# When the last step of the attention state's second half is put down: both head pairs together, or one pair at a time

## The chip, the cores and the metric

The kernel runs on one core of a Trainium2 chip. The core has engines with a queue of instructions each: TensorE (PE, matrix products into PSUM banks), VectorE (DVE), ScalarE (ACT), GpSimd (POOL) and SyncE (SP), whose queue issues nearly all of this kernel's transfers. They wait for each other through semaphores. The metric is the device time of one execution in microseconds (us).

## The reference

One block of a streaming encoder, for 1024 tokens of width 1024 and 16 meta tokens ahead of them: a mixer of a multi-scale pooling branch and a chunked, gated linear attention (GLA, 4 heads, chunks of 64), merged by sigmoid gates, and then an MLP with a squared ReLU. The part that bears on the change:

```python
def gla_chunk_step(S, inp):
    qc, kc, vc, ac = inp
    ...
    o = jnp.einsum('bhts,bhsv->bhtv', scores, vc) + jnp.einsum('bhtk,bhkv->bhtv', qc * jnp.exp(b), S)
    ...
    return S_new, o

    o = gla_chunked(q, k, v, log_a)
    o = rmsnorm(o, gla_norm.reshape(GLA_HEADS, GLA_DV)) * jax.nn.silu(r).reshape(B, L, GLA_HEADS, GLA_DV)
    y_b = jnp.einsum('blc,cd->bld', o.reshape(B, L, GLA_VAL), w_gla_out)
    m = jax.nn.sigmoid(ga) * y_a + jax.nn.sigmoid(gb) * y_b
    return jnp.einsum('bld,de->ble', m, w_out)
```

All of it is float32.

## The kernel before

A float32 operand is split into a rounded part and a remainder, and every product is made of three matmuls (`mm3`, L280 to L282: rounded by rounded, and the two mixed ones). Weights go through a ring of two slots (`Ring`, W1): a load from DRAM into one of two raw buffers (L118, on SP), the rounding on ACT (L84, writes `w1h`), the remainder on DVE (L85, writes `w1l`).

The program has two parts, `one` (norm, projections, the pooling branch) and `rest` (GLA across the chunks, merge, output projection, MLP). The change is in `gla()`, the first long step of `rest`. There the 1024 tokens are two halves of 512, and the 4 heads two pairs. `across(p, half)` is a generator for one pair in one half. It yields four times, so it has five steps: turning the keys (L1124), the state's updates (L1130, L1136), the scores by the values (L1144), the queries by the states with the norm (L1154 to L1164), and the last one, which the change is about (L1167 to L1175): eight transposes on PE (L1168) into two PSUM banks (`m2` for pair 0, `sc` for pair 1), the product with the gate `sr` on DVE (L1169), the rounding into `yg` on ACT (L1171) and its remainder on DVE (L1172). Each of these DVE and ACT operations is 128x1024.

Between the steps PE does filler work, which `drive` hands out in units of three matmuls of 128x512, at a cost of 0.64 each: `pour(us)` takes units until their costs reach `us`, and a surplus is carried over. The filler is first the products of the pooling branch, `ya_block`, and then `yb_block(j, 0)`, y_b of half 0. Block j (of four) has the weights of 256 columns of w_gla_out and makes the output tiles d = 2j and 2j + 1, twelve matmuls each, into one of three `mm` PSUM banks in turn. I call these tiles d0 to d7. DVE leaves a tile's bank with L1095 (gate times product), adds the pooling branch (L1096), ACT rounds the sum (L1099), and DVE makes the remainder (L1100). The gates and the pooling branch come in small buffers (`o`, `t1`, `c`, loads L1037).

At the end of `gla()` the rest of the filler is done. `merge_open` then reuses the memory, and `yb_block(j, 1)` follows, half 1's tiles in the order of blocks 2, 3, 0, 1. Blocks 2 and 3 still lie in the two ring slots; block 0's and 1's weights are loaded again. Between them the weights w_out come in four loads (L1237, into `acc`) with a rounding (L1238) and a remainder (L1239), since the output projection (`out_tile`) begins after half 1's d0 and d1.

PE runs in the order in which the program is written. The other engines' orders are set by a scheduler that works from PE's order.

Of the kernel before, what the change touches and what calls it, by code (L numbers as in the profile page):

```python
# [122 lines left out]
def kernel(  # L123
# [30 lines left out]
    def bank(tag):  # L154
        if tag == "sc":
            sc_n[0] += 1
            return two("sc")[:, sc_n[0] % 2]
        return psp[tag].tile([P, 512], F32, name=f"b_{tag}", tag=tag)

    def two(tag):  # L160

        if tag in ("sc", "gs"):
            if tag not in wide:
                wide[tag] = psp[tag].tile([P, 2, 512], F32, name=f"b_{tag}", tag=tag)
            return wide[tag]
        return psp[tag].tile([P, 2, 512], F32, name=f"b_{tag}", tag=tag)
# [45 lines left out]
    def f32(ap):  # L212
        return ap.bitcast(F32)
# [11 lines left out]
    def inv_sqrt(ss, n, inv, bias=None):  # L225

        rows, cols = ss.shape[0], n
        k = inv_sqrt.k = (inv_sqrt.k + 1) % 2
        v, y = stat[2 * k][:rows, 0:cols], stat[2 * k + 1][:rows, 0:cols]
        t = stat[2 * k][:rows, 8 : 8 + cols]  # L230
        act.activation(y, ss, ACT.Ln, scale=inv, bias=eps_t[:rows] if bias is None else bias)
        dve.tensor_scalar(v, ss, inv, EPS if bias is None else bias, ALU.mult, ALU.add)
        act.activation(y, y, ACT.Exp, scale=-0.5)
        if cols == 1:
            dve.scalar_tensor_tensor(t, v, y, y, ALU.mult, ALU.mult)
        else:
            dve.tensor_tensor(t, v, y, ALU.mult)
            dve.tensor_tensor(t, t, y, ALU.mult)
        dve.tensor_scalar(t, t, -0.5, 1.5, ALU.mult, ALU.add)
        dve.tensor_tensor(ss, y, t, ALU.mult)  # L240
        return ss
# [74 lines left out]
    def drive(steps, late=0.0):  # L316

        due = late
        for n, (ring, aps, fn) in enumerate(steps):
            if fn is not start:  # L320
                for r in rings:
                    if late and r.loaded >= r.used + len(aps):
                        r.ask()
                    else:
                        r.top_up()
            wbs = [ring.views.pop(ring.used + i) for i in range(len(aps))] if ring else []
            held = len(aps)
            if ring:
                ring.used += held
            for cost in fn(*wbs) or ():  # L330
                if cost == "keep":
                    held = 0
                    continue
                if cost == "free":
                    if ring:
                        ring.done, held = ring.done + held, 0
                    else:
                        W1.done += 1
                    due = late if n < 3 else 1.0
                    for r in rings:  # L340
                        r.ask()
                        if not late:
                            r.split()
                    continue
                if late and cost != "wait":
                    due -= cost
                    if due <= 0:
                        for r in rings:
                            r.split(pin=True)
                yield cost  # L350
            if ring:
                ring.done += held
# [155 lines left out]
    def quad(a):  # L508
        return a.rearrange("p (k c) -> p k c", k=4)
# [384 lines left out]
    def part(i):  # L894
        return slice(i * CH, (i + 1) * CH)
# [15 lines left out]
    def dec_of(p, half):  # L911
        return decs[:, (2 * half + p) * NC : (2 * half + p + 1) * NC]
# [99 lines left out]
    def fetch(p, half):  # L1012
        if half < 2:
            nc.sync.dma_start(S["gi"][p], gi_dram[p, half])
# [96 lines left out]
    def across(p, half):  # L1111


        gi, kt, W = S["gi"][p], S["kt"][p], S["W"][p]
        scc = gi[:, 0].rearrange("p (e j t) -> p e j t", e=2, j=4)
        kl, qe = gi[:, 1], gi[:, 2]
        v = S["v"][:, p, 4 * half : 4 * half + 4].rearrange("p j (e c) -> p j e c", e=2)
        dec = dec_of(p, half)
        first = S["S"][:, half, p]
        wide2 = lambda: two("sc" if p else "m2")  # L1120
        sr = S["sr"][p].rearrange("p e t -> p (e t)")
        b = quad(bank("ms") if p == 0 else wide2()[:, 0])
        for j in range(4):
            pe.transpose(b[:, j], kl[:, j * P : (j + 1) * P], ident)  # L1124
        act.activation(kt, b, ACT.Copy)
        yield 1.4
        kv = wide2().rearrange("p u (j c) -> p u j c", j=4)
        for j in range(4):
            for u, e in ((0, 0), (1, 1), (1, 0), (0, 1)):
                pe.matmul(  # L1130
                    kv[part(e), u, j], kt[part(u), j, part(e)], v[part(u), j, e], start=True, stop=True,
                    tile_position=(u * CH, e * CH),
                )
        states = [first] + [W[:, c] for c in range(NC - 1)] + ([S["S"][:, 1, p]] if half == 0 else [])
        for c, dst in enumerate(states[1:]):
            dve.scalar_tensor_tensor(dst, states[c], dec[:, c : c + 1], kv[:, c % 2, c // 2], ALU.mult, ALU.add)  # L1136
        nc.sync.dma_start(S["sr"][p], r_dram[2 * p : 2 * p + 2, half].rearrange("h p t -> p h t"))
        yield 5.0

        o = wide2().rearrange("p e (j c) -> p e j c", j=4)  # L1140
        for j in range(4):
            for e in range(2):
                for u in range(2):
                    pe.matmul(  # L1144
                        o[part(u), e, j], scc[part(u), e, j], v[part(u), j, e], start=j == 0, stop=False,
                        tile_position=(u * CH, u * CH), skip_group_check=True,
                    )

        dve.tensor_copy(rms[p][:, :2], o[:, :, 3, P - 1])
        yield 0.8  # L1150
        for j in (3, 0, 1, 2):
            for e, u in ((0, 0), (1, 1), (1, 0), (0, 1)):
                c = 2 * j + u
                pe.matmul(  # L1154
                    o[part(u), e, j], qe[part(e), part(c)], states[c][part(e)], start=False, stop=True,
                    tile_position=(e * CH, u * CH), skip_group_check=True,
                )
        fetch(p, half + 1)
        on, o = S["on"][p], o.rearrange("p e j c -> p (e j) c")
        act.activation(on, o, ACT.Square)  # L1160
        ss = rms[p]
        dve.tensor_reduce(ss, on, AX.X, ALU.add)
        rs = inv_sqrt(ss, 8, 1.0 / P)
        dve.tensor_tensor(on, o, rs[:, :, None].broadcast_to([P, 8, P]), ALU.mult)  # L1164
        yield 8.0
        b = wide2().rearrange("p e (j c) -> p (e j) c", j=4)
        for j in range(8):  # L1167
            pe.transpose(b[:, j], on[:, j], ident)  # L1168
        dve.tensor_tensor(sr, b.rearrange("p a c -> p (a c)"), sr, ALU.mult)  # L1169
        yh, yl = (S["yg"][half][:, n, 2 * p : 2 * p + 2].rearrange("p e t -> p (e t)") for n in range(2))  # L1170
        act.activation(yh, sr, ACT.Copy)  # L1171
        dve.tensor_tensor(yl, sr, f32(yh), ALU.subtract)  # L1172
        done.add((p, half))
        if {(0, half), (1, half)} <= done:
            done.add(("o", half))  # L1175

    def gla():
        W1.far = len(W1.queue)
        filler = drive(fill, 5.0)

        owed = [0.0]

        def pour(us):
            owed[0] += us
            while owed[0] > 0:
                cost = next(filler, None)
                if cost is None or cost == "wait":
                    owed[0] = 0.0
                    return
                owed[0] -= cost  # L1190

        pour(OPENING)
        for half in range(2):
            live = [across(p, half) for p in range(2)]
            while live:
                waits = [(g, next(g, None)) for g in live]
                live = [g for g, w in waits if w is not None]
                pour(max([w for _, w in waits if w is not None], default=2.0) * PACE)
        for _ in filler:
            pass  # L1200

    step(rest, gla)


# [426 lines left out]
```

## Time and profile before

| | |
|---|---|
| Time, median of 3 runs | 1226.18 us (1223.92 to 1226.18) |
| The profiled execution's own time | 1222.42 us |
| Its span, first to last instruction | 1220.6 us |
| PE busy | 1204.6 us (99%) |
| DVE busy | 838.9 us (69%) |
| ACT busy | 572.3 us (47%) |
| Granted TensorE clock, mean | 0.999 |

A time in a row of the timeline is a start, counted from the span's start, and the number behind it is the duration. Matmuls overlap: a row of 0.39 us does not keep the next one from starting 0.23 us later, so the pace is read from the starts. An arrow in brackets names what ended an idle time; where an instruction waits for several, it is the one that came last by the profile. SPq rows are issues of transfers; the transfer itself lands some microseconds later.

### The profile page before, as it was taken

To read this page: it belongs to the slowest core of one execution; us is meant where nothing else is said; L and a number is where in the kernel's file an instruction comes from. 1 tells how busy PE (TensorE), PEld (TensorE's weight loads), DVE (VectorE), ACT (ScalarE), POOL (GpSimd) and SP (SyncE) were. 2 spreads that over 40 slices of the span, in tenths; PEclk is the share of its full clock that TensorE was granted. 3 is DMA by queue.
4 is the path that set the end of the run, shared out by engine and by line. 5 is a ranking of instruction groups with operands and counts; after the bars stand their busy time and mean duration, and the time that the engine had idled before them with its cause. 6 is when DMAs were issued, how large, how long until landed. Compare 5 with 4: busy or idle time off the path is not lost.

```text
span 1220.6 us, 18363 instructions
## 1 busy us (share of the span) xinstructions
PE 1204.6 (99%) x6807; PEld 996.5 (82%) x6807; DVE 838.9 (69%) x1381; ACT 572.3 (47%) x1009; POOL 75.7 (6%) x96
## 2 busy tenths in 40 slices
PE   9999999999999999999999999999999999999997
PEld 7988977777778887888778888888888888888886
DVE  7536557565777569735887677676775887887686
ACT  8536444444456224314655455454554444444544
POOL 0000053322230000000000000000000000000000
PEclk9999999999999999999999999999999999999999
DMA  8213334435338967821244454444569973333532
GB/s 261 73 35 114 104 95 137 141 104 166 96 121 291 326 222 248 296 67 69 104 139 156 143 162 152 148 155 145 173 228 322 334 246 104 96 95 96 171 96 87
DMA packets 153355, 192.76 MB, mean 158 GB/s; under 512 B 12177, under 2 KB 88225, under 8 KB 153266
## 3 DMA queue, kind: packets, MB, share of 16 engines
q1 hardware_dynamic: 153266, 191.59, 48.9%
q8 instruction: 53, 0.87, 0.3%
q14 instruction: 36, 0.29, 0.1%
HBM read 128.62 MB, written 62.93 MB: 157 GB/s over the span
## 4 chain that ended last, share of the span: by engine, by line
PE 89%; DVE 4%; DMA 3%; ACT 1%; issue 1%; POOL 0%; SPq 0%; DVEq 0%; ACTq 0%; POOLq 0%
PE b_mm L280 7%; PE b_mm L282 7%; PE b_mm L281 7%; PE b_y L280 6%; PE b_y L282 6%; PE b_y L281 6%; PE b_oa L281 5%; PE b_oa L282 5%; PE b_oa L280 5%; PE b_z L280 4%; PE b_z L282 4%; PE b_z L281 4%; PE b_sc L280 4%; PE b_ob L281 4%; PE b_ob L282 4%; PE b_ob L280 4%
## 5 line engine op out<-in xcount | busy, mean ns | idle before, releaser
L685 ACT ACTIVATE w1h<-raw 128x512 fp32r<-128x512 f32 x106 | 65.9, 623 | 57.9 <-PE b_y L281 25.3
L686 DVE TENSOR_TENSOR w1l<-raw,w1h 128x512 fp32r<-128x512 f32 x106 | 72.5, 685 | 20.5 <-ACT w1h L685 20.5
L280 PE MATMUL b_sc<-th,w1h 128*128 128x512 f32 x216 | 85.7, 397 | 0.7 <-ACT u2p L1414 0.7
L280 PE MATMUL b_z<-th,w1h 128*128 128x512 f32 x216 | 85.3, 395 | 0.6 <-DVE c L804 0.4
L281 PE MATMUL b_sc<-tl,w1h 128*128 128x512 f32 x216 | 84.9, 393 | 0.0
L281 PE MATMUL b_z<-tl,w1h 128*128 128x512 f32 x216 | 84.3, 391 | 0.4 <-DVE tl L1300 0.4
L282 PE MATMUL b_sc<-th,w1l 128*128 128x512 f32 x216 | 84.5, 391 | 0.0
L685 ACT ACTIVATE w1h<-fs 128x512 fp32r<-128x512 f32 x81 | 51.1, 631 | 71.1 <-PE b_y L281 33.2
L282 PE MATMUL b_z<-th,w1l 128*128 128x512 f32 x216 | 84.2, 390 | 0.0
L686 DVE TENSOR_TENSOR w1l<-fs,w1h 128x512 fp32r<-128x512 f32 x81 | 56.9, 702 | 25.9 <-ACT w1h L685 25.8
L280 PE MATMUL b_mm<-th,w1h 128*128 128x512 f32 (+1 forms) x208 | 72.2, 347 | 0.0
L281 PE MATMUL b_mm<-tl,w1h 128*128 128x512 f32 (+1 forms) x208 | 71.1, 342 | 0.0
L282 PE MATMUL b_mm<-th,w1l 128*128 128x512 f32 (+1 forms) x208 | 71.1, 342 | 0.0
L685 ACT ACTIVATE w1h<-bt 128x512 fp32r<-128x512 f32 x46 | 29.1, 632 | 70.9 <-issue 43.9
L1490 DVE TENSOR_TENSOR bt<-w,w 128x512 f32<-128x512 f32 x80 | 54.7, 684 | 0.7 <-DMA w<-in_w_ff_dram 0.6
L280 PE MATMUL b_mm<-wo,th 128*128 128x512 f32 x128 | 50.4, 394 | 0.0
L282 PE MATMUL b_mm<-wo,tl 128*128 128x512 f32 x128 | 50.0, 390 | 0.0
L281 PE MATMUL b_mm<-wo,th 128*128 128x512 f32 x128 | 49.9, 390 | 0.0
L280 PE MATMUL b_y<-wo,w1h 128*128 128x512 f32 x128 | 49.9, 389 | 0.0
L282 PE MATMUL b_y<-wo,w1l 128*128 128x512 f32 x128 | 49.8, 389 | 0.0
L281 PE MATMUL b_y<-wo,w1h 128*128 128x512 f32 x128 | 49.8, 389 | 0.0
L686 DVE TENSOR_TENSOR w1l<-bt,w1h 128x512 fp32r<-128x512 f32 x46 | 31.8, 691 | 25.6 <-ACT w1h L685 25.6
(405 smaller groups left out, 3331.8 us busy)
## 6 DMA issues: line engine op xcount, KB each, us to landing
hf_dram<-h SPq DMA_DIRECT2D x112, 256.0 KB, 2.1
raw<-hf_dram SPq DMA_DIRECT2D x112, 256.0 KB, 2.6
w<-in_w_ff_dram SPq DMA_DIRECT2D x64, 256.0 KB, 4.7
raw<-in_w_in_dram SPq DMA_DIRECT2D x22, 512.0 KB, 4.7
raw<-in_w_ff_dram SPq DMA_DIRECT2D x16, 512.0 KB, 4.2
rawx<-in_w_ff_dram SPq DMA_DIRECT2D x16, 512.0 KB, 4.3
rawp<-in_w_in_dram SPq DMA_DIRECT2D x10, 512.0 KB, 4.3
xs<-in_x_dram SPq DMA_DIRECT2D x8, 512.0 KB, 4.9
```

What stands on the lines that cost most here:

```text
L280: pe.matmul(ps, ah, bh, start=first and i == 0, stop=False, skip_group_check=more)
L281: pe.matmul(ps, ah, bl, start=False, stop=False, skip_group_check=more)
L282: pe.matmul(ps, al, bh, start=False, stop=last and i == n - 1, skip_group_check=more)
L685: act.activation(hi, a, ACT.Copy)
L686: dve.tensor_tensor(lo, a, f32(hi), ALU.subtract)
L1490: dve.tensor_tensor(bt, w, S["w2"][q[3:]][:, i], ALU.add if q[2] == "+" else ALU.subtract)
```

## The change

In half 1 the generators' first four steps are put down as before, for both pairs at a time. For the fifth, a branch takes pair 0's step, then filler for 4.0, then pair 1's step, then none. Before, both pairs' last steps stood together, with 2.0 x 1.3 = 2.6 of filler behind them. Half 0 is as it was, and no instruction is added or removed.

```diff
         for half in range(2):
-            live = [across(p, half) for p in range(2)]
+            live, parts = [across(p, half) for p in range(2)], 4
             while live:
+                if half and not parts:
+                    for g, us in zip(live, (4.0, 0.0)):
+                        next(g, None)
+                        pour(us)
+                    break
+                parts -= 1
                 waits = [(g, next(g, None)) for g in live]
                 live = [g for g, w in waits if w is not None]
                 pour(max([w for _, w in waits if w is not None], default=2.0) * PACE)
```

The lines behind it move by six, so L1237 to L1239 of the kernel before are L1243 to L1245 of the changed one.

On PE, at the end of `gla()` (half 0's d2 ends ahead of the first row; `b_m` and `b_sc` are the banks of the two pairs' transposes):

```order
@@ -2135,5 +2135,4 @@
 L282 MATMUL b_mm<-yg_3837,w1l 128x512
 L1168 MATMUL b_m_4556<-ident,on_3865 128x128 x8
-L1168 MATMUL b_sc<-ident,on_3869 128x128 x8
 L280 MATMUL b_mm<-yg_3837,w1h 128x512
 L281 MATMUL b_mm<-yg_3837,w1h 128x512
@@ -2154,4 +2153,5 @@
 L281 MATMUL b_mm<-yg_3837,w1h 128x512
 L282 MATMUL b_mm<-yg_3837,w1l 128x512
+L1168 MATMUL b_sc<-ident,on_3869 128x128 x8
 L280 MATMUL b_mm<-yg_3837,w1h 128x512
 L281 MATMUL b_mm<-yg_3837,w1h 128x512
```

Pair 1's transposes have moved back by 18 matmuls: d3 and the first half of d4 now stand between the pairs.

On DVE at the same place, before. `sr0` and `sr1` are the two pairs' gates; the banks are numbered by when they were given out: 4585 is d3, 4605 is d4, 4624 is d5; the last row is the remainder of block 3's weights:

```order
L1169 TENSOR_TENSOR sr1_3861<-b_sc_230,sr1_3861 128x1024
L1172 TENSOR_TENSOR yg1_3833<-sr0_3857,yg1_3833 128x1024
L1096 TENSOR_TENSOR o_3841<-o_3841 128x512
L1172 TENSOR_TENSOR yg1_3833<-sr1_3861,yg1_3833 128x1024
L1100 SCALAR_TENSOR_TENSOR tl0_140<-o_3841,th0_136 128x512
L1095 SCALAR_TENSOR_TENSOR o_3841<-o_3841,b_mm_4585 128x512
L1095 SCALAR_TENSOR_TENSOR t1_1015<-t1_1015,b_mm_4605 128x512
L1096 TENSOR_TENSOR o_3841<-o_3841,t1_1015 128x512
L1096 TENSOR_TENSOR t1_1015<-t1_1015 128x512
L1095 SCALAR_TENSOR_TENSOR c_1011<-c_1011,b_mm_4624 128x512
L1100 SCALAR_TENSOR_TENSOR tl0_140<-o_3841,th0_136 128x512
L85 TENSOR_TENSOR w1l_132<-raw1_124,w1h_128 128x1024
```

And now, from pair 0's L1169 on, where 4574 is d3:

```order
L1169 TENSOR_TENSOR sr0_3857<-b_m2_4556,sr0_3857 128x1024
L1096 TENSOR_TENSOR o_3841<-o_3841 128x512
L1095 SCALAR_TENSOR_TENSOR o_3841<-o_3841,b_mm_4574 128x512
L1172 TENSOR_TENSOR yg1_3833<-sr0_3857,yg1_3833 128x1024
L1100 SCALAR_TENSOR_TENSOR tl0_140<-o_3841,th0_136 128x512
L1096 TENSOR_TENSOR o_3841<-o_3841,t1_1015 128x512
L1169 TENSOR_TENSOR sr1_3861<-b_sc_230,sr1_3861 128x1024
L1100 SCALAR_TENSOR_TENSOR tl0_140<-o_3841,th0_136 128x512
L85 TENSOR_TENSOR w1l_132<-raw1_124,w1h_128 128x1024
L1172 TENSOR_TENSOR yg1_3833<-sr1_3861,yg1_3833 128x1024
```

Pair 1's two operations now stand behind d3's sum (the L1096 with `t1`), and the last L1172 behind block 3's L85; the L1095 of d4 and d5 follow behind that. On ACT, likewise, pair 1's L1171 now follows block 3's L84 and the L1099 of d2 and d3, where it was ahead of all three.

On DVE at the second place, in half 1, before. 4658 is half 0's d7; 4727, 4780 and 4746 are half 1's d4, d6 and d5:

```order
L1095 SCALAR_TENSOR_TENSOR o_3841<-o_3841,b_mm_4658 128x512
L1096 TENSOR_TENSOR o_3841<-o_3841 128x512
L1239 TENSOR_TENSOR wo0_4699<-acc_4703,wo0_4699 128x1024 x2
L1100 SCALAR_TENSOR_TENSOR tl0_140<-o_3841,th0_136 128x512
L1239 TENSOR_TENSOR wo0_4699<-acc_4703,wo0_4699 128x1024 x2
L85 TENSOR_TENSOR w1l_132<-raw0_120,w1h_128 128x1024
L1095 SCALAR_TENSOR_TENSOR t1_4711<-t1_4711,b_mm_4727 128x512
L1095 SCALAR_TENSOR_TENSOR o_4715<-o_4715,b_mm_4780 128x512
L1096 TENSOR_TENSOR t1_4711<-t1_4711 128x512
L1095 SCALAR_TENSOR_TENSOR t1_4711<-t1_4711,b_mm_4746 128x512
```

And now:

```order
L1096 TENSOR_TENSOR o_3841<-o_3841 128x512
L1245 TENSOR_TENSOR wo0_4699<-acc_4703,wo0_4699 128x1024
L1100 SCALAR_TENSOR_TENSOR tl0_140<-o_3841,th0_136 128x512
L1245 TENSOR_TENSOR wo0_4699<-acc_4703,wo0_4699 128x1024 x2
L85 TENSOR_TENSOR w1l_132<-raw0_120,w1h_128 128x1024
L1095 SCALAR_TENSOR_TENSOR o_4715<-o_4715,b_mm_4780 128x512
L1095 SCALAR_TENSOR_TENSOR t1_4711<-t1_4711,b_mm_4727 128x512
L1245 TENSOR_TENSOR wo0_4699<-acc_4703,wo0_4699 128x1024
L1096 TENSOR_TENSOR t1_4711<-t1_4711 128x512
```

The L1095 of d6 (4780) and that of d4 (4727) have changed places, and the last w_out remainder has moved behind both. On SP the first three w_out loads have moved behind the load L118 of block 1's weights for half 1, and the fourth behind the four loads L1037 of half 1's first gates. Behind half 1's tiles the engines' orders are the same.

## The prediction

> **What bounds the kernel now.** The page's first part comes first:
>
> ```profile
> PE 1204.6 (99%) x6807; PEld 996.5 (82%) x6807; DVE 838.9 (69%) x1381; ACT 572.3 (47%) x1009; POOL 75.7 (6%) x96
> ```
>
> TensorE (PE) is busy in 99% of the span, so its products are the floor: their number does not change here, and an edit of their order can only win or lose PE's idle time. PE's own waits tell where that is; the two longest that lie near the change, of the whole run, are these (total, times, longest):
>
> ```profile
> PE b_mm L280 <- ACT w1h L84: 2.3, 1, 2.3
> PE b_mm L282 <- DVE w1l L85: 0.6, 1, 0.6
> ```
>
> Both happen once, at 475 us, ten microseconds behind the step that is changed. The timeline of PE from there (start, duration; in brackets the idle time before, and what ended it):
>
> ```profile
> 464.68 1.03 PE L1168 MATMUL b_m<-ident,on 128*128 128x128 f32 x8
> 465.55 1.04 PE L1168 MATMUL b_sc<-ident,on 128*128 128x128 f32 x8
> 466.34 0.48 PE L280 MATMUL b_mm<-yg,w1h 128*128 128x512 f32 x1
> 466.66 0.40 PE L281 MATMUL b_mm<-yg,w1h 128*128 128x512 f32 x1
> ...
> 474.38 0.39 PE L282 MATMUL b_mm<-yg,w1l 128*128 128x512 f32 x1
> 477.09 0.50 PE L280 MATMUL b_mm<-yg,w1h 128*128 128x512 f32 x1 [2.33 <-ACT w1h L84]
> 477.43 0.40 PE L281 MATMUL b_mm<-yg,w1h 128*128 128x512 f32 x1
> 478.42 0.50 PE L282 MATMUL b_mm<-yg,w1l 128*128 128x512 f32 x1 [0.59 <-DVE w1l L85]
> 478.75 0.40 PE L280 MATMUL b_mm<-yg,w1h 128*128 128x512 f32 x1
> ...
> 491.47 0.39 PE L282 MATMUL b_mm<-yg,w1l 128*128 128x512 f32 x1
> 492.08 0.50 PE L280 MATMUL b_mm<-yg,w1h 128*128 128x512 f32 x1 [0.22 <-DVE t L1095]
> ```
>
> The transposes of both head pairs stand together at 464.68. Then come 36 products (half 0's d3 to d5), and at 477.09 d6, the first of block 3, which lacks its weights. From 478.75 to 491.47 there are 56 steps in 12.72 us, so a product takes 0.227 us when nothing is missing. Without waits 478.75 would have been 474.38 + 4 x 0.227 = 475.29, so this first place costs 3.46 us. The second place, 492.08 (half 1's d7), came 0.61 us after the product before it, and its follower 0.1 us late as after every stop: it costs 0.38 + 0.11 = 0.49 us.
>
> Why the weights were late stands on ScalarE (ACT) and VectorE (DVE):
>
> ```profile
> 468.97 2.19 ACT L1171 ACTIVATE yg<-sr 128x1024 fp32r<-128x1024 f32 x2 [2.68 <-DVE sr L1169]
> 475.46 0.63 ACT L1099 ACTIVATE th<-o 128x512 fp32r<-128x512 f32 x1 [2.90 <-DVE o L1096]
> 476.00 1.04 ACT L84 ACTIVATE w1h<-raw 128x1024 fp32r<-128x1024 f32 x1
> ```
>
> ```profile
> 466.58 1.22 DVE L85 TENSOR_TENSOR w1l<-raw,w1h 128x1024 fp32r<-128x1024 f32 x1
> 467.72 1.22 DVE L1169 TENSOR_TENSOR sr<-b_m,sr 128x1024 f32<-128x1024 f32 x1
> 468.86 1.21 DVE L1169 TENSOR_TENSOR sr<-b_sc,sr 128x1024 f32<-128x1024 f32 x1
> 470.06 1.23 DVE L1172 TENSOR_TENSOR yg<-sr,yg 128x1024 fp32r<-128x1024 f32 x1
> 471.20 0.68 DVE L1096 TENSOR_TENSOR o<-o 128x512 f32<-128x512 f32 x1
> 471.81 1.22 DVE L1172 TENSOR_TENSOR yg<-sr,yg 128x1024 fp32r<-128x1024 f32 x1
> ...
> 474.74 0.69 DVE L1096 TENSOR_TENSOR o<-o,t 128x512 f32<-128x512 f32 x1
> ...
> 477.14 1.22 DVE L85 TENSOR_TENSOR w1l<-raw,w1h 128x1024 fp32r<-128x1024 f32 x1
> ```
>
> The rounding L84 is queued on ACT behind L1099 of d3, which waits for DVE's sum at 474.74; that sum stands behind the four wide operations of the two head pairs. DVE has no idle time in these rows: its starts are 1.14 us apart behind a wide operation (467.72 to 468.86) and 0.60 behind a narrow one (471.20 to 471.81). A wait passes in about 0.05 us (L84 ends at 477.04, PE starts at 477.09).
>
> **The change, place one.** Pair 0's transposes stay; 18 products later come pair 1's. No instruction is added or removed, so the engines' busy sums stay. One more break between transposes and products is made; what a break costs is bounded by 466.34 to 466.66, 0.32 instead of 0.227: 0.1 us, taken.
>
> On DVE, by the order and these spacings: sr of pair 0 at 467.72 as before, d2's sum 468.86, d3's L1095 469.46, yg of pair 0 at 470.06, d2's L1100 471.20, d3's sum 471.80 instead of 474.74. It ends at 472.49; ACT, free since the single yg, does L1099 at 472.5, and L84 follows 0.54 later, as 475.46 to 476.00 shows: 473.06 to 474.10 instead of 477.04. Meanwhile DVE does sr of pair 1 (472.40; its transposes ended near 470.8), L1100 (473.54) and L85 at 474.14, which ends at 475.36 instead of 478.36.
>
> PE reaches d6 at 474.38 + 0.23 + 0.1 = 474.7: the rounded weights are there, so the 2.33 us wait goes. Next late is the remainder: the third product would start at 475.15 and starts at 475.41; the fourth follows after 0.33 (478.42 to 478.75) at 475.74 instead of 478.75. Place one wins 3.0 us; with no remainder wait it would be 3.4, and 2.7 if DVE slips by half a narrow operation.
>
> **Place two.** What is paid stands in the order of DVE near 491: these rows of before are DVE's, ACT's and the issuing queue SP's there, and the last two lines give the times from issue to landing, of the four w_out loads and of the eight loads of x (L1226) behind them, all of 512 KB.
>
> ```profile
> 485.07 2.35 DVE L1239 TENSOR_TENSOR wo<-acc,wo 128x1024 fp32r<-128x1024 f32 x2
> 487.34 0.68 DVE L1100 SCALAR_TENSOR_TENSOR tl<-o,th 128x512 fp32r<-128x512 f32 x1
> 487.94 2.35 DVE L1239 TENSOR_TENSOR wo<-acc,wo 128x1024 fp32r<-128x1024 f32 x2
> 490.21 1.21 DVE L85 TENSOR_TENSOR w1l<-raw,w1h 128x1024 fp32r<-128x1024 f32 x1
> 491.35 0.68 DVE L1095 SCALAR_TENSOR_TENSOR t<-t,b_mm 128x512 f32<-128x512 f32 x1
> 491.94 0.68 DVE L1095 SCALAR_TENSOR_TENSOR o<-o,b_mm 128x512 f32<-128x512 f32 x1
> ```
>
> ```profile
> 483.85 2.01 ACT L1238 ACTIVATE wo<-acc 128x1024 fp32r<-128x1024 f32 x2 [0.76 <-DMA acc<-in_w_out_dram]
> 488.95 1.06 ACT L84 ACTIVATE w1h<-raw 128x1024 fp32r<-128x1024 f32 x1 [0.66 <-PE b_mm L281]
> ```
>
> ```profile
> 473.09 0.38 SPq L1237 DMA_DIRECT2D acc<-in_w_out_dram  x1
> 474.04 0.94 SPq L1237 DMA_DIRECT2D acc<-in_w_out_dram  x2
> ```
>
> ```profile
> DMA to landing us min/median/max: 4.8/6.3/6.9
> ...
> DMA to landing us min/median/max: 5.3/6.9/8.7
> ```
>
> Half 1's d7 takes the PSUM bank that its d4 leaves: there are three, and 491.35, the L1095 that ended 0.05 before 492.08, is d4's. In the new order d6's L1095 stands ahead of d4's, and it can start only when d6's last product is done. That product is the one right before d7, so the wait is certain. d6's last product starts at 475.74 + 12.72 = 488.46 and ends 0.39 later (474.38's duration), at 488.85; two narrow operations follow, to 488.88 + 0.60 + 0.68 = 490.16, and d7 starts at 490.21 instead of 488.69. With 0.11 behind the stop this costs 1.63 us at least, 1.14 more than the 0.49 now.
>
> It may be more, because the w_out loads move too. Their first issue waits for the last yg (471.81 + 1.23 = 473.04, then 473.09). That operation now stands behind L85, at 475.28 to 476.51, so the loads go out from 476.55, 3.46 us later. At 6.3 us the first lands at 482.85. ACT then rounds (1.0 each by 483.85's row, and one L1099 between) until 486.4 and does L84 until 487.45. DVE has by then done eleven narrow operations behind the last yg, 476.42 + 11 x 0.60 = 483.0, and subtracts behind ACT: 483.9, L1100 at 485.0, 485.6, 486.8, L85 at 487.9, d6's L1095 at 489.06, d4's at 489.66 to 490.34. So d7 starts at 490.39, and the place costs 1.81, 1.3 more than now. A landing of 6.9 shifts this by 0.6, to 1.9 more. I take 1.3, the median's; the fourth load, now behind four loads of half 1's gates, is subtracted after d4's L1095, and no product before the output tiles needs it.
>
> The Trainium skill, page "DMA: Bandwidth & Descriptors", section "Anatomy of one DMA — SWDGE (gpsimd) path", fits a DMA of GpSimd's queue as some 2.0 us plus its bytes over 436 GB/s, an estimate of 3.2 us for 512 KB. The trace disagrees, with 4.8 to 6.9 on SP's queue; by the page the loads would never be last, and the sum would be 1.9 instead of 1.7.
>
> **The sum.** 3.0 - 1.3 = 1.7 us won, between 2.7 - 1.9 = 0.8 and 3.4 - 1.1 = 2.3. Behind 500 us the order is as before, and the products move up as a body. The profiled execution took 1222.42 us for a span of 1220.6, and becomes 1220.7. It is faster than the three runs shown (1223.92 to 1226.18); from their median, 1226.18, the forecast is 1224.5. A difference of 0.2%, 2.45 us, is about what this kernel's runs can tell from none.
>
> **The rivals.** First, the second place costs nothing, because the bank of d7 is not the one that I read out of 492.08's wait. Against it is the 0.05 us between the two rows; for it only that a releaser is inferred. Then 3.0 is won: 1223.2.
>
> Second, the gain is given back later.
>
> ```profile
> 480.00:490.00 10.00, 10.00 (x46) 8.29 (x45) 8.91 (x11) 6.35 (x8) 0.00 (x0) 1.00 0.72 236
> ...
> 560.00:620.00 60.00, 58.38 (x285) 47.78 (x284) 49.76 (x96) 38.45 (x79) 0.00 (x0) 1.00 0.21 79
> ```
>
> Of these windows the columns are the length and then PE, weight loads, DVE, ACT and GpSimd, with clock and DMA behind. PE idles 1.62 us between 560 and 620. Were a transfer behind it bound to no product, PE would meet it 1.7 us sooner and wait as long: 1226.2. Against it: DMA's share there is 0.21, so loads wait for buffers that products release.
>
> Third, it is slower: the loads of w_out, now behind pair 1's last operation and and behind L118's 512 KB of weights on SP, land so late that d7's stop outgrows the old one. Each microsecond of landing beyond 6.3 is one of PE; the point is 1.7 more, 8.0 us. At 8.7 the loss would be 2.4 - 1.7 = 0.7: 1226.9. The rows' worst is 6.9.
>
> Fourth, that longer stop also slows the clock behind it. The window from 480 above shows 1.00 right behind the 2.33 us of idle time that there is now, so nothing in this trace speaks for it. The stop would be 3.4 us and more; products at half speed for as long again cost half of that, 1.7: 1228.6. The Trainium skill, page "TensorE: Matmul & The Clock Gate", section "Part 1: The HAM clock gate (the "warmup" mystery)", says that the clock halves after an idle window of about 3.4 us; no run here shows such a stop.
>
> **How the numbers follow.** Forecast 0.60, first rival 0.17, second 0.14, third 0.07, fourth 0.02. The forecast's bounds stay within 0.2%, but medians of three runs that spread over 2.26 us do not: 0.14 of its 0.60 I count as faster, with the first rival 0.31. Slower by over 0.2% are the fourth rival and 0.04 of the third and second, again for the runs' spread: 0.06; the rest, 0.63, is the same. The range reaches from the lowest run less the forecast's better part, 1223.92 - 1.9 = 1222.0, to the third rival's 1226.9.
>
> **What would show it.** In the new profile L84 ahead of d6 ends near 474.1, and PE's wait there is a few tenths, for L85. At half 1's d7 PE waits 1.5 to 1.7 us for d4's L1095, which follows d6's. The w_out loads leave SP near 476.5. If d6 still waits for L84, or d7 does not wait, or PE's idle time between 500 and 620 grows beyond 1.6 us, the prediction is wrong in that step.

## The result, and the profile after

The changed kernel took 1222.73 us (median of 12 runs, 1219.79 to 1222.97), the kernel before, run beside it, 1226.18 (12 runs, 1221.92 to 1226.74). The ratio is 0.9973, with a 95% interval of 0.9963 to 0.9984: faster by 0.27%, 3.45 us by the medians, where 1.7 were forecast. One run of this study, of the version e2_before_filled below, took 3258.12 us at a mean granted clock of 0.365, and no ratio here counts it. The profiled execution after took 1222.77 us for a span of 1221.0, which is no less than the 1222.42 and 1220.6 of the profile before; the reason stands in the first microseconds. These are TensorE's rows for the first products of the program, in the trace of before and in that of after:

```profile
5.17 2.14 PE L460 MATMUL b_mm<-um,xm 1*128 1x512 f32 x4
7.24 1.98 PE L449 MATMUL b_ms<-xr 128*128 128x512 f32 x4
```

```profile
5.16 3.78 PE L460 MATMUL b_mm<-um,xm 1*128 1x512 f32 x4
8.87 3.78 PE L449 MATMUL b_ms<-xr 128*128 128x512 f32 x4
12.45 0.99 PE L266 MATMUL b_sc<-ident,us 128*128 128x128 f32 x4
```

The same four products take 2.0 us in the one and 3.8 in the other: a run starts at about half its later pace, and the full pace comes some 5 us into the span or some 13. (The column of the granted clock reads 1.00 in both starts, so the pace is all that these traces show of it.) Either kernel has both kinds of start: before's second trace, below, has the late one, and the changed kernel's second the early one. The late start shifts all that follows by 2.5 to 3 us, which must be taken off before two traces are compared. So positions below are measured from pair 0's transposes (464.68 before, 467.24 after). The line of busy times and PE's waits near the change, after:

```profile
PE 1207.9 (99%) x6807; PEld 997.2 (82%) x6807; DVE 838.9 (69%) x1381; ACT 572.0 (47%) x1009; POOL 75.5 (6%) x96
```

```profile
PE b_mm L280 <- DVE o L1095: 1.2, 1, 1.2
...
PE b_mm L282 <- DVE w1l L85: 0.2, 1, 0.2
```

PE's idle time fell from 1220.6 - 1204.6 = 16.0 us to 1221.0 - 1207.9 = 13.1. Not all of these 2.9 us are the change's: from 460 to 505 us PE's idle time fell from 3.14 us to 1.32, by 1.8, and most of the rest (0.85) lies in the first 30 us, where the starts differ. Near the change, the wait of 2.3 us for the rounded weights (L84) is gone, that for their remainder is 0.2 instead of 0.6, and the wait at half 1's d7 has grown from 0.2 to 1.2. The timeline of PE after, in the same places as before:

```profile
467.24 1.03 PE L1168 MATMUL b_m<-ident,on 128*128 128x128 f32 x8
472.21 1.04 PE L1168 MATMUL b_sc<-ident,on 128*128 128x128 f32 x8
...
477.44 0.39 PE L281 MATMUL b_mm<-yg,w1h 128*128 128x512 f32 x1
477.98 0.50 PE L282 MATMUL b_mm<-yg,w1l 128*128 128x512 f32 x1 [0.15 <-DVE w1l L85]
478.31 0.39 PE L280 MATMUL b_mm<-yg,w1h 128*128 128x512 f32 x1
...
491.04 0.39 PE L282 MATMUL b_mm<-yg,w1l 128*128 128x512 f32 x1
492.59 0.50 PE L280 MATMUL b_mm<-yg,w1h 128*128 128x512 f32 x1 [1.17 <-DVE o L1095]
...
500.88 0.39 PE L280 MATMUL b_mm<-wo,th 128*128 128x512 f32 x1
```

In before's trace the last of these, the first product of the output projection, stands here:

```profile
500.42 0.39 PE L280 MATMUL b_mm<-wo,th 128*128 128x512 f32 x1
```

To d6's fourth product it is 478.75 - 464.68 = 14.07 us before and 478.31 - 467.24 = 11.07 after: 3.00 won. From pair 0's transposes to the output projection it is 500.42 - 464.68 = 35.74 and 500.88 - 467.24 = 33.64: 2.10 of that is kept. This stretch is the yardstick for the experiments. Behind it nothing is given back: from that product to the end of the span it is 1220.6 - 500.42 = 720.18 us before and 1221.0 - 500.88 = 720.12 after. Between 560 and 620 us PE is busy for 58.50 us of 60 after, 58.38 before.

ACT and DVE after, at place one, the first issues of the w_out loads on SP, and DVE at place two:

```profile
475.08 0.63 ACT L1099 ACTIVATE th<-o 128x512 fp32r<-128x512 f32 x1 [1.98 <-DVE o L1096]
475.62 1.04 ACT L84 ACTIVATE w1h<-raw 128x1024 fp32r<-128x1024 f32 x1
```

```profile
479.12 1.41 SPq L1243 DMA_DIRECT2D acc<-in_w_out_dram  x3
```

```profile
474.36 0.69 DVE L1096 TENSOR_TENSOR o<-o,t 128x512 f32<-128x512 f32 x1
474.97 1.22 DVE L1169 TENSOR_TENSOR sr<-b_sc,sr 128x1024 f32<-128x1024 f32 x1
476.10 0.68 DVE L1100 SCALAR_TENSOR_TENSOR tl<-o,th 128x512 fp32r<-128x512 f32 x1
476.70 1.23 DVE L85 TENSOR_TENSOR w1l<-raw,w1h 128x1024 fp32r<-128x1024 f32 x1
...
488.45 2.35 DVE L1245 TENSOR_TENSOR wo<-acc,wo 128x1024 fp32r<-128x1024 f32 x2
490.72 1.22 DVE L85 TENSOR_TENSOR w1l<-raw,w1h 128x1024 fp32r<-128x1024 f32 x1
491.86 0.68 DVE L1095 SCALAR_TENSOR_TENSOR o<-o,b_mm 128x512 f32<-128x512 f32 x1
492.46 0.68 DVE L1095 SCALAR_TENSOR_TENSOR t<-t,b_mm 128x512 f32<-128x512 f32 x1
...
494.79 0.68 DVE L1095 SCALAR_TENSOR_TENSOR t<-t,b_mm 128x512 f32<-128x512 f32 x1
```

L84 ends at 476.66, which is 474.10 on the clock of before's trace; there it ended at 477.04. At place two PE goes on at 492.59, 0.05 us after d6's L1095 (491.86 + 0.68 = 492.54) and while d4's (492.46) still runs; d5's follows at 494.79.

So the profiles agree with a gain of 2.1 us, and the medians say 3.45. The times fall into groups that make the difference. The 91 runs of before that stood beside the others in this study lie in three: 18 between 1221.9 and 1223.2 us, 28 between 1223.6 and 1225.1, 45 between 1226.0 and 1227.3. The 22 runs of the changed kernel lie in two, 10 from 1219.8 to 1220.9 and 12 from 1222.6 to 1223.3, and the two are as far apart as the two starts above. The medians of the two lowest groups, 1222.5 and 1220.4, are 2.1 apart, and the profile of before was of the lowest. What before has besides is its third group, with half of its runs. Nor is its middle group simply the late start, which 2.1 us above the changed kernel's would lie at some 1225.0: only 5 of its 28 runs lie above 1224.5.

### The profile page after: what moved, and what is told of

Same layout as the page of the kernel before. It is cut to its first block, busy times and chain, and to the rows that moved or that the text cites. A ratio compares the mean times of both kernels' runs of the same rounds, so it can differ in the third digit from the quotient of the medians.

```text
span 1221.0 us, 18366 instructions
## 1 busy us (share of the span) xinstructions
PE 1207.9 (99%) x6807; PEld 997.2 (82%) x6807; DVE 838.9 (69%) x1381; ACT 572.0 (47%) x1009; POOL 75.5 (6%) x96
## 4 chain that ended last, share of the span: by engine, by line
PE 89%; DVE 4%; DMA 2%; ACT 2%; issue 2%; POOL 0%; SPq 0%; POOLq 0%; ACTq 0%; DVEq 0%
PE b_mm L280 7%; PE b_mm L282 7%; PE b_mm L281 7%; PE b_y L280 6%; PE b_y L282 6%; PE b_y L281 6%; PE b_oa L282 5%; PE b_oa L281 5%; PE b_oa L280 5%; PE b_z L280 4%; PE b_z L282 4%; PE b_z L281 4%; PE b_sc L280 4%; PE b_ob L281 4%; PE b_ob L282 4%; PE b_ob L280 4%
```

## The experiments

All were run beside the kernel before. The stretch is that from pair 0's transposes to the first product of the output projection, in the profiled execution of each.

| Run | Stretch, us | Wait at d6, us | Wait at half 1's d7, us | Ratio to before (95% interval) |
|---|---|---|---|---|
| before | 35.74 | 2.33 + 0.59 | 0.22 | |
| after | 33.64 | 0.15 | 1.17 | 0.9973 (0.9963 to 0.9984) |
| e1_before_again | 37.27 | 2.33 + 0.60 | 0.23 | 0.9993 (0.9982 to 1.0004) |
| e2_before_filled | 35.70 | 0.59 | 0.22 | 0.9988 (0.9977 to 1.0000) |
| e8_half_filled | 37.33 | 1.19 + 0.60 | 0.22 | 0.9992 (0.9980 to 1.0005) |
| e4_evac_later | 33.59 | 0.20 | 0.81 | 0.9969 (0.9958 to 0.9980) |
| e6_pour_two | 35.62 | 2.18 + 0.59 | 0.22 | 1.0003 (0.9989 to 1.0017) |
| e7_pour_six | 35.54 | 0.41 | 0.47 | 0.9986 (0.9975 to 0.9997) |
| e3_after_swapped | 33.42 | 0.15 | none | 0.9969 (0.9956 to 0.9983) |
| e5_both_places | 32.22 | 0.15 | none | 0.9965 (0.9951 to 0.9979) |
| e9_after_again | 33.67 | 0.15 | 1.15 | 0.9969 (0.9958 to 0.9980) |
| e10_both_again | 32.18 | 0.15 | none | 0.9965 (0.9952 to 0.9977) |

**Where the rest of the median's gain is: the kernel before, profiled again.** There is no edit.

> The kernel before, unchanged, for its own spread: its runs so far lie in three groups, 1222, 1224 and 1226.5 us, those of the changed kernel in two, 1220 and 1222.8, so that like groups differ by about 2.0 and the medians by 3.45. Two theories on the missing 1.5 us. Clock theory: the 2.3 us stop of TensorE at half 0's d6 halves the clock for some 3.4 us in those runs of before that take 1226.5; a profile of such a run shows a granted clock well under 1.00 in the 10 us behind d6, and the waits as in the profile that there is (2.3 + 0.6 us). Wait theory: in such a run the clock stays at 1.00 and one of the waits, at d6 or elsewhere, is 1.5 to 2 us longer. A profile at 1222 tells neither apart.

The profiled execution was one of 1226.84 us. Its windows (columns as in the prediction; the clock is the third figure from the right) and PE's rows around half 0's d6:

```profile
480.00:485.00 5.00, 4.31 (x11) 3.17 (x12) 3.26 (x5) 1.19 (x3) 0.00 (x0) 0.66 0.90 317
485.00:490.00 5.00, 5.00 (x24) 4.13 (x23) 3.67 (x6) 2.23 (x3) 0.00 (x0) 1.00 0.44 159
```

```profile
467.69 1.03 PE L1168 MATMUL b_m<-ident,on 128*128 128x128 f32 x8
...
480.09 0.50 PE L280 MATMUL b_mm<-yg,w1h 128*128 128x512 f32 x1 [2.33 <-ACT w1h L84]
...
481.42 0.80 PE L282 MATMUL b_mm<-yg,w1l 128*128 128x512 f32 x1 [0.60 <-DVE w1l L85]
482.02 0.63 PE L280 MATMUL b_mm<-yg,w1h 128*128 128x512 f32 x1
482.44 0.63 PE L281 MATMUL b_mm<-yg,w1h 128*128 128x512 f32 x1
...
484.58 0.48 PE L280 MATMUL b_mm<-yg,w1h 128*128 128x512 f32 x1
...
504.96 0.39 PE L280 MATMUL b_mm<-wo,th 128*128 128x512 f32 x1
```

The waits are those of the first profile, to a hundredth. But right behind them the granted clock is 0.66 in the mean of five microseconds, the products lie 0.43 us apart instead of 0.227 (482.02 to 482.44), and at 484.6 the fall is over. The stretch is 504.96 - 467.69 = 37.27 us, 1.53 more than in the first profile; with the 3.01 by which its transposes come later (467.69 against 464.68) that makes 4.54, and the spans differ by 1225.1 - 1220.6 = 4.5. The clock theory holds for this run, the wait theory falls: the runs of the third group, half of before's, pay for the stop at d6 twice, once as idle time and once as slow products behind it. The middle group mostly seems to do so too, with the early start (a run of e8_half_filled, below, that was profiled at 1223.93 us had both); with its 23 runs under 1224.5 it would be three quarters of before's.

**Filling the stop without curing it.** Ten products that nobody reads stand ahead of d6; one order changes, PE's, by that one row.

```diff
                 gl, ml = take("b", d, h)
+                if d == 6 and not h:
+                    f = bank("ms")
+                    for _ in range(10):
+                        pe.matmul(f, yg[:, 0, 0, :P], yg[:, 0, 0], start=True, stop=True)
                 b = bank("mm")
```

> The kernel before with ten more products of 128x512 (2.3 us, into a PSUM bank that nobody reads) on TensorE right before half 0's d6, so that its wait is filled and not cured; no other engine's order changes. Clock theory: with the stop at d6 down to some 0.15 + 0.6 us the runs of 1226.5 are gone, and the median falls to 1224.6 or less, 0.998 to 0.999 of before. Wait theory: the time stays, 0.999 to 1.001, and the group of 1226.5 stays too.

```profile
474.88 2.43 PE L1089 MATMUL b_ms<-yg 128*128 128x512 f32 x10
...
478.69 0.50 PE L282 MATMUL b_mm<-yg,w1l 128*128 128x512 f32 x1 [0.59 <-DVE w1l L85]
```

The stretch is 35.70, as before, so nothing is cured; yet the eleven runs that count lie from 1222.2 to 1223.3 (seven) and from 1224.6 to 1225.3 (four), and none at 1226. The ratio of 0.9988 is as the clock theory said, but its interval ends at 1.0000, and the kernel before against itself gave 0.9993: what speaks for the theory is that no run lies between 1223.3 and 1224.6 or at 1226, where 68 of before's 91 runs are.

**How much of a stop it takes.** Five such products instead of ten.

> The kernel before with five products ahead of half 0's d6 instead of ten, so that some 1.2 + 0.6 us of the stop are left of 2.3 + 0.6. The end of the stop does not move. If the clock falls only behind a stop of some 2 us and more, the runs of 1226.5 are gone as with ten products, 0.9985 to 0.999; if a stop of half the length is enough, the three groups stay, 1.000. In the changed kernel a stop of 1.2 us stands at place two and no run shows a third group, which speaks for the first.

```profile
477.00 0.50 PE L280 MATMUL b_mm<-yg,w1h 128*128 128x512 f32 x1 [1.19 <-ACT w1h L84]
...
478.33 0.50 PE L282 MATMUL b_mm<-yg,w1l 128*128 128x512 f32 x1 [0.60 <-DVE w1l L85]
...
479.33 0.63 PE L282 MATMUL b_mm<-yg,w1l 128*128 128x512 f32 x1
479.76 0.63 PE L280 MATMUL b_mm<-yg,w1h 128*128 128x512 f32 x1
```

My guess of some 2 us falls: behind 1.19 + 0.60 us, with two products between, the clock falls too, in this profile of 1223.93 us, an early start with a slow stretch (37.33). The three groups are all there, four of 12 runs at 1226.

**Is it DVE's queue or PE's order?** DVE, ACT and SP run here in the changed kernel's order, row for row, while PE does both pairs' transposes together, as before.

```diff
             pe.transpose(b[:, j], on[:, j], ident)
+        if p and half:
+            yield 0.0
+        with tc.issue_after(summed[3].ins) if p and half else ExitStack():
-        dve.tensor_tensor(sr, b.rearrange("p a c -> p (a c)"), sr, ALU.mult)
+          dve.tensor_tensor(sr, b.rearrange("p a c -> p (a c)"), sr, ALU.mult)
...
-                    for g, us in zip(live, (4.0, 0.0)):
-                        next(g, None)
-                        pour(us)
+                    for g in live:
+                        next(g, None)
+                    pour(4.0)
+                    next(live[1], None)
```

> The order of the change on VectorE, ScalarE and SyncE, row for row, but TensorE's order as before: pair 1's transposes stand right behind pair 0's again, and only their evacuation is put behind d3's sum. My theory: the queue of VectorE is the whole cause, TensorE's separation of the two groups of transposes is nothing: 0.997 of before, as the changed kernel within 0.2 us, L84 ahead of d6 in time and d7's stop at 1.4 us. Rival: the separation on TensorE is what counts, since pair 1's evacuation is ready only when its transposes have come: 1.000 of before.

```profile
467.22 1.03 PE L1168 MATMUL b_m<-ident,on 128*128 128x128 f32 x8
468.09 1.04 PE L1168 MATMUL b_sc<-ident,on 128*128 128x128 f32 x8
477.96 0.50 PE L282 MATMUL b_mm<-yg,w1l 128*128 128x512 f32 x1 [0.20 <-DVE w1l L85]
```

33.59 us, and the changed kernel's ratio. That the transposes are apart on PE is worth nothing. (d7 waits for 0.81 us here instead of 1.17, but from there to the output projection it takes 8.57 us instead of 8.29, so that nothing is left of it.) Which of the other three orders counts, this run alone does not tell; before's rows do: ACT stood idle for 2.90 us until DVE's sum was there, so what the change does is to let d3's sum pass pair 1's wide operations on DVE. The reverse, a split on PE that leaves all four wide operations of DVE ahead of d3's sum, is the next one, with `pour(2.0)` between the pairs.

> The split of the change with 2.0 us of filler between the two head pairs instead of 4.0: TensorE's transposes are apart, 9 or so products, but on VectorE all four wide operations still stand ahead of d3's sum, as before. Queue theory: nothing is won at d6, whose wait stays at 2.3 + 0.6 us, the clock falls behind it in the same share of runs, and the ratio is 1.000. Rival: being apart on TensorE is what helps; then half or more of the gain, 0.9985 or less.

```profile
477.01 0.50 PE L280 MATMUL b_mm<-yg,w1h 128*128 128x512 f32 x1 [2.18 <-ACT w1h L84]
478.34 0.50 PE L282 MATMUL b_mm<-yg,w1l 128*128 128x512 f32 x1 [0.59 <-DVE w1l L85]
```

The waits stay (2.18 us for 2.33), 7 of the 12 runs lie above 1226, and the ratio is 1.0003: the queue theory holds. Half of the split is not half of the gain, because an order has steps.

**A larger split**, `pour(6.0)`, which sends the w_out loads out later still.

> The split with 6.0 us of filler instead of 4.0: pair 1's operations go two more tiles back on VectorE, and the w_out loads, which wait for its last one, leave about 482 instead of 478 us. Theory of the two places: place one as in the changed kernel, without the wait for the rounded weights; place two worse, d7 waits some 2.2 us instead of 1.2 since the remainders of w_out come 4 us later and d4's L1095 stands behind them: 0.998 of before. Rival: what is late at place two is d4's gate load (issued at 488.6) and not w_out; then as the changed kernel, 0.997.

```profile
489.94 0.50 PE L280 MATMUL b_mm<-yg,w1h 128*128 128x512 f32 x1 [0.47 <-DVE t L1095]
...
500.57 0.47 PE L280 MATMUL b_mm<-wo,th 128*128 128x512 f32 x1 [2.15 <-issue]
```

```profile
495.77 2.36 DVE L1245 TENSOR_TENSOR wo<-acc,wo 128x1024 fp32r<-128x1024 f32 x2
...
498.65 1.22 DVE L85 TENSOR_TENSOR w1l<-raw,w1h 128x1024 fp32r<-128x1024 f32 x1
499.79 0.68 DVE L1095 SCALAR_TENSOR_TENSOR o<-o,b_mm 128x512 f32<-128x512 f32 x1
```

Neither theory had the place right. d7 waits for 0.47 us only, and 2.15 us are lost at the output projection's first product. The releaser is named "issue"; by the rows of DVE it is most likely d7's L1095, which ends at 500.47, 0.10 us before PE goes on, behind the late remainders of w_out and an L85, and so gives a bank back late. The stretch is 35.54, hardly less than before's 35.74, but 7 of the 12 runs lie under 1223 and none over 1225.6. With about the same idle time in other places (0.41 + 0.47 + 2.15 = 3.03 us; before 2.33 + 0.59 + 0.22 = 3.14) the clock falls seldom, if at all.

**Curing place two.** In the trace after, half 1's d4 and d5 read the buffers `t`, whose loads leave SP at 488.6, and d6 those that are loaded from 483.3. The changed kernel with the two groups the other way round:

```diff
-        lend("t1", "o")
+        lend("o", "t1")
```

> The changed kernel with the two buffer groups of half 1's gates lent in the other order, so that d4 and d5 get the group whose loads go out first (483.3 instead of 488.6 us), and their L1095 stand ahead of three of the four w_out remainders. My theory: d7 then takes d4's bank without a wait, the 1.43 us of place two are won, and the ratio to before goes from 0.9972 to about 0.996 (1221.3 if before is 1226.2). Rival: the remainders of w_out, now later by two narrow operations and more, are missed by the first output tile, and the gain shows up as a wait there: 0.997 as the changed kernel.

```profile
494.49 2.35 DVE L1245 TENSOR_TENSOR wo<-acc,wo 128x1024 fp32r<-128x1024 f32 x2
496.76 0.68 DVE L1095 SCALAR_TENSOR_TENSOR t<-t,b_mm 128x512 f32<-128x512 f32 x1
```

```profile
497.49 0.50 PE L280 MATMUL b_mm<-yg,w1h 128*128 128x512 f32 x1 [0.92 <-DVE t L1095]
```

d7's wait is gone, and d1, 24 products later, waits 0.92 us for the bank of d6, whose L1095 now stands behind two remainders of w_out. Of 1.4 us 0.2 is left. The rival was right in kind, with another place than it named. So these two remainders go behind the L1095 of d6 and d7 as well (the buffers swapped as above):

```diff
             act.activation(wo[:, 0], r, ACT.Copy)
+            if not ch and kk > 1:
+                late.append((wo, r))
+                return
             dve.tensor_tensor(wo[:, 1], r, f32(wo[:, 0]), ALU.subtract)
...
+    def late_remainders():
+        with tc.issue_after(freed[7, 1].ins):
+            for wo, r in late:
+                dve.tensor_tensor(wo[:, 1], r, f32(wo[:, 0]), ALU.subtract)
...
     yb(3)
+    step(rest, late_remainders)
     yb(0)
```

> As the run with swapped buffers, in which the 1.4 us of place two went and 1.0 us came back 24 products later (half 1's d1 waited 0.92 us for d6's L1095, behind two w_out remainders at 494.49 and 496.76), and now those two remainders stand behind the L1095 of d6 and d7. My theory: d1's wait goes too, all 1.4 us of place two are won against the changed kernel, like groups at 1218.8 and 1221.3, ratio to before 0.996 or a little less. Rival: VectorE is full there (10.0 of 10 us busy from 490 to 500), so that whatever is put back is missed by the next in line, the first output tile; then the ratio stays at 0.997.

```profile
495.00 1.27 DVE L1095 SCALAR_TENSOR_TENSOR t<-t,b_mm 128x512 f32<-128x512 f32 x2
...
499.13 1.22 DVE L1255 TENSOR_TENSOR wo<-acc,wo 128x1024 fp32r<-128x1024 f32 x1
```

The stretch is 32.22, all 1.42 us of it won, and PE waits nowhere between 480 and 530. It and the changed kernel were then run side by side.

> The changed kernel, unchanged, beside the version with both places cured, so that the two share a chip and the runs of before. Clock theory: no run of it takes longer than 1223.3, no window between 465 and 510 us shows a granted clock under 1.00, and the ratio to before is 0.997, while before again spreads from 1222 to 1227 us. Wait theory: now and then a run of it, too, is 1.5 us above its two groups (1220.3 and 1222.8).

> The version with both places cured (swapped buffers, two remainders put back) once more, beside the changed kernel. If the stretch from pair 0's transposes to the first product of the output projection stays at 32.2 us, against 33.6 in the changed kernel, it is 1.4 us faster: ratio to before about 0.996, 0.001 under the changed kernel's of the same call. If something behind 560 us takes part of it back, 0.5 to 1.0 us.

The stretches came out again, 33.67 and 32.18. The changed kernel had no run over 1223.3 and a clock of 1.00 from 465 to 510 us, as the clock theory expects. The medians of the two versions' runs (1220.52 and 1221.70) are no comparison, since six of ten runs of the one and one of six of the other had the early start. Taken start by start over all their runs, the version with both places cured has its medians at 1219.1 and 1221.8, the changed kernel at 1220.4 and 1222.9: 1.0 to 1.3 us better, and the fastest version here. The ratios, 0.9965 and 0.9969, have intervals that overlap.

## Why the prediction was right, and where not

**Place one** held in every term: L84 ends at 474.10 on before's clock (forecast 474.10), PE then lacks only the remainder, for 0.15 us, and 3.00 us are won (3.0). The two experiments on the order (e4 and e6) show that the cause is the one given.

**Place two** held in kind; its size was 1.43 us instead of 1.81: (492.59 - 491.04 - 0.227) + 0.11. That d6's L1095 stands first, and that the w_out loads leave 3.47 us later (479.12 - 2.56 = 476.56, forecast 476.55), came true. The step that failed is that d7 takes d4's bank. In this order it goes on behind the first of the two operations, d6's, so one narrow operation (0.60) counts and not two; DVE came to d6's L1095 0.24 later than forecast (491.86 - 2.56 = 489.30 for 489.06), which takes part of that back, and 0.94 is lost instead of 1.3. That it is d6's bank follows from the rows: of the three banks d4's was left at 492.46 + 0.68 = 493.14 and d5's at 494.79 + 0.68 = 495.47, both after PE had begun d7 at 492.59. By what rule a tile gets its bank was not tried. Nor could d4's L1095 have come much sooner: its gates are loaded so late that in one run (e4) DVE itself waits for them for 0.75 us.

**The sum**, 1.7, measured 2.10 on the stretch and 2.1 between the lowest groups. Of the rivals, the first (place two free) falls with the 1.17 us at d7, the second with the 720.1 us behind the stretch, against 720.2, and the third with loads that landed in 6.4 us (the median of the four w_out loads after).

**The median** is where the forecast was furthest off, 1224.5 against 1222.73. The failing step is "from their median, 1226.18, the forecast is 1224.5": it carried the difference of one profiled execution over to runs that were not like it. The profile was of the lowest group, the runs with an early start and no slow stretch, one run in five. The fourth rival had the mechanism and the price (1.7; measured 1.53), but put it on the new stop, and "nothing in this trace speaks for it" was true of the trace and not of the kernel. The stop that trips the clock was the old one, and the change takes it away: about 2.1 us in every run, and 1.5 more in those that fell. That the median of 1222.73 still lies in the range is partly luck: the range's lower end, 1222.0, was drawn from the lowest of three runs, and not with this gain in mind. The three times shown were a hint: a spread of 2.26 us in before, and a profile 1.5 below the lowest.

## What to carry to other kernels

A wait for an operand is often the queue of another engine: look for what stands ahead there and what of it could come later, and remember that whoever is passed is missed next, until nothing needs it in time. Price a stop of TensorE with the slow products that may follow it, and where a kernel's runs fall into groups, profile a run of the common one before a single trace is taken for the kernel.

## What the runs showed of the hardware

The granted clock falls to half behind a stop shorter than I had thought: 2.33 + 0.60 us with two products between, and also 1.19 + 0.60 us. The fall lasts for some 3.4 us (in before's second trace the clock's mean is 0.66 over 5 us, which is 0.34 x 5 / 0.5 = 3.4 us of half clock) and costs 1.5 to 1.6. It comes in a part of the runs only. The Trainium skill, page "TensorE: Matmul & The Clock Gate", section "Part 1: The HAM clock gate (the "warmup" mystery)", speaks of an idle window of about 3.4 us and of a window that runs free of the program. The length of the slow stretch and its presence in some runs alone agree with that; that a whole window must be idle does not. What else decides is open: single stops of 1.2 us (the changed kernel, 22 runs) made no third group, and one of 2.15 us (`pour(6.0)`, 12 runs) at most three runs that could be such (1224.4 to 1224.5).
